# Attention scores in three float32r passes, with the operands cut beforehand and reciprocals spread by GpSimd

## The chip, the cores and the metric

The kernel runs on one core of one Trainium2 chip. The metric is the device time of one execution in microseconds (us). All times of the profile count from the start of its span. Engines go by the names of the profile: PE (TensorE, matmuls), PEld (its weight loads), DVE (VectorE), ACT (ScalarE), POOL (GpSimd) and SP (SyncE, which issues most DMAs).

## What is computed

One block of a transformer trunk in float32: 1024 latent tokens on a grid of 16 rows by 64 columns and 256 context tokens, width 1024. A modulated RMS norm is followed by a projection into a pooling half and queries, keys and values of 8 heads of 64. The attention, cut to what matters here, is

```python
s_loc = jnp.einsum('bnqhd,brnkhd->bhnqrk', q_r, k_b) * scale
s_loc = jnp.where(col_mask, s_loc + bias, -jnp.inf)      # 8 x 16 neighbourhood, learned bias
s_ctx = jnp.einsum('bnqhd,bkhd->bhnqk', q_r, k_ctx) * scale
p = softmax(concatenate([s_loc, s_ctx]))
o = p_loc @ v_local + p_ctx @ v_ctx
```

Then come the output projection with a gated residual, a second modulated norm and a squared-ReLU MLP of width 4096 with another gated residual.

## The kernel before

Nearly every large product is made of float32r matmuls: an operand x is cut into a high part (x rounded to float32r, a cast on ACT) and a low part (x minus the high part, a subtraction on DVE), and a product takes three passes, high by high, high by low, low by high (`three`, L198 to L200). The large products are further arranged in seven block products P1 to P7 in place of eight (`seventh`, `last_query`), whose results are combined on DVE and ACT (`kept_product`, L907 to L925). The exceptions are products of the attention, which run directly on float32 operands.

Ahead of the attention the projections of keys and queries run in 24 numbered steps, two per product; an order of instructions on each engine is fixed by the program text. The tables of biases (`tables(j)`, L869 on) are built on POOL: a DMA on SP's queue brings the windows of the learned biases (`U`), and twelve POOL operations of 128x128 (L883) subtract them from a mask, for the two heads of group j. The table of group 0 is built in step 20; that of group j + 1 in the iteration of unit (j, 2), all twelve operations at once.

The attention is a loop over 32 units (j, m): j is a pair of heads, m a tile of 128 queries (two grid rows). Unit number i is 8j + m. The loop is pipelined by hand; iteration i issues, in this order (each engine works in the order of the text):

- tables, weight loads, `weighed(i-4)` (L1070, DVE: values times reciprocals), and at fixed i other work of the block: `mod_gate` (i = 4), `column_sums` (i = 5 for `sc`, i = 8 for `sh`), `mixed_split` (i = 8, 16, 24), `weight_split` (i in `HALVES` = 12, 14, 20, 22 and later);
- `scores(i)` (L971 on): one matmul per head for the local keys (384 columns; 256 at the image edges m = 0 and 7) and one per head for the 256 context keys, L984. A head has 64 rows, and the two heads of a unit use the upper and the lower half of PE's rows. Then one DVE instruction per head (L998) adds the bias table and takes the minimum `nm` that the softmax needs;
- `turn(i-2)` (L1026): PE transposes. The first two are of `rb`, the reciprocals of the softmax sums spread over 64 columns per head; then come the probabilities. `fifth_kept` (ACT, L1040) copies the result of the first ones to `px`;
- the exponentials of unit i (ACT, L1007) around the copies of the turned probabilities to `pt` (L1045, one half on ACT, one on DVE);
- for i below 2, the last projection product of the queries (`last_query("P4", i)`);
- `share(i-1)`: the reciprocal of the sums (L1011) and its spread into `rb` (L1013), both on DVE;
- `values(i-3)` (L1060): PE.

`column_sums` (L620 on) sums a modulation row on PE, copies the result on ACT (L621), stores it to memory in four DMAs (`mod_out`, L253) and reads it back, spread over the partitions, in one DMA (L623). These DMAs are issued by POOL, and L623 waits there until the four have landed. Accumulating DMAs (`add_to`, L188) are issued by POOL too; they bring the results of finished heads together (`y`, `ss`, `f`).

The scores have two sets of two PSUM banks, so the scores of unit i + 1 can start on a head's bank only when L998 of that head of unit i is done.

## Time and profile before

| what | value |
|---|---|
| median of 3 runs | 1032.79 us (1032.4 to 1032.83) |
| span of the profiled execution | 1030.8 us, about 2 us less than the runs; its own time isn't among the shown ones |
| PE busy | 1017.8 us, 99% of the span |
| attention loop, from the first score to the output projection | 219 to 322.4 us |
| scores' matmuls, L984 | 128 in the program, 256 records, 4% of the chain that ended last |
| reciprocals and spreads, L1011 and L1013 | 32 each, on DVE, median 227 ns a spread |
| table operations on POOL, L883 | 48 |

A float32 matmul of the program appears as two records, one for each of its passes; a float32r matmul as one. Durations of matmuls overlap, since they are pipelined: what one takes of PE's time is read from the distance of two starts. In lists of groups, the columns are the line, the engine, the operation, output and inputs, the shapes and a count; then busy time and mean duration of one; then the idle time of the engine just ahead of them and who ended it. "L623 <-DMA gsc" in brackets with a time is a wait and what ended it.

### The profile page before, as it was taken

The numbers are of one execution on the slowest core, as the hardware profiler recorded it, in microseconds if no ns is written. First come the engines' busy times: TensorE is split into PE (matmuls) and PEld (weight loads), VectorE is DVE, ScalarE is ACT, GpSimd is POOL, SyncE is SP. The second block draws the span as 40 slices with busy tenths as digits, with TensorE's granted clock in tenths as the row PEclk, the third lists the DMA queues.
The fourth block names the chain that finished last, engine by engine and source line by source line (L and its number), as shares of the span: only waits on it lengthen the run. The fifth ranks groups of instructions, "written<-read, shape, count | busy, mean of one in ns | idle before, by whom it ended". The sixth has DMA issues, their size and how long they took to land.

```text
span 1030.8 us, 15588 instructions
## 1 busy us (share of the span) xinstructions
PE 1017.8 (99%) x5782; PEld 834.2 (81%) x5782; DVE 751.8 (73%) x1187; ACT 543.7 (53%) x941; POOL 110.7 (11%) x168
## 2 busy tenths in 40 slices
PE   8999999999999999999999999999999999999997
PEld 6788888877887888888888888888888888888885
DVE  5588767858996587878998887855766666547576
ACT  7573255328887556776655544555543334334431
POOL 3011200244311311310000000000000000000001
PEclk9999999999999999999999999999999999999999
DMA  9999798632337866795786666637967766555556
GB/s 343 332 255 338 246 265 296 204 86 80 72 95 194 203 180 200 253 237 168 267 269 210 204 210 214 205 122 241 327 220 271 248 226 220 202 180 189 176 182 211
DMA packets 123132, 222.68 MB, mean 216 GB/s; under 512 B 9456, under 2 KB 55152, under 8 KB 123056
## 3 DMA queue, kind: packets, MB, share of 16 engines
q1 hardware_dynamic: 96560, 171.14, 50.4%
q0 software_dynamic: 9360, 19.58, 9.5%
q10 hardware_dynamic: 17136, 30.97, 8.0%
q8 instruction: 45, 0.74, 0.3%
q14 instruction: 31, 0.25, 0.1%
HBM read 168.16 MB, written 52.45 MB: 214 GB/s over the span
## 4 chain that ended last, share of the span: by engine, by line
PE 95%; DMA 2%; ACT 1%; DVE 1%; issue 0%; SPq 0%; DVEq 0%; POOLq 0%; ACTq 0%
PE pu L449 4%; PE S L984 4%; PE pa L1060 3%; PE phv L198 3%; PE phz L198 3%; PE phx L198 3%; PE pyx L198 3%; PE phx L200 3%; PE phv L199 3%; PE phx L199 3%; PE pyx L199 3%; PE pyx L200 3%; PE pyv L199 3%; PE pyv L198 3%; PE pyz L199 3%; PE pyz L198 3%
## 5 line engine op out<-in xcount | busy, mean ns | idle before, releaser
L1007 ACT ACTIVATE sp<-sp,nm 128x640 f32<-128x640 f32 (+1 forms) x64 | 51.4, 803 | 20.0 <-DVE nm L998 19.6
L1577 ACT ACTIVATE c<-c 128x512 f32<-128x512 f32 x48 | 30.3, 632 | 47.0 <-DVE c L1697 28.2
L146 ACT CAST wpS<-S 128x512 fp32r<-128x512 f32 x64 | 38.7, 616 | 26.4 <-PE phv L200 9.2
L198 PE MATMUL phx<-thB,wpA 128*128 128x512 f32 x128 | 50.2, 392 | 0.0
L200 PE MATMUL phx<-thB,wpA 128*128 128x512 f32 x128 | 49.8, 389 | 0.0
L199 PE MATMUL phx<-tlB,wpA 128*128 128x512 f32 x128 | 49.8, 389 | 0.0
L152 DVE TENSOR_TENSOR wpS<-S,wpS 128x512 fp32r<-128x512 f32 x64 | 43.4, 685 | 8.3 <-ACT wpS L146 8.3
L998 DVE CUSTOM_DVE_ANT_0 sp<-S,tab 128x640 f32<-128x640 f32 (+1 forms) x56 | 42.9, 803 | 8.8 <-PE S L984 7.3
L1578 ACT ACTIVATE c<-c 128x512 f32<-128x512 f32 x48 | 30.3, 631 | 15.1 <-DVE sa L1660 12.3
L140 POOL TENSOR_TENSOR ry<-vy,nhalf 128x1 f32<-128x1 f32 x8 | 5.9, 740 | 280.7 <-DVE vy L138 280.7
L198 PEld LDWEIGHTS phx<-thB,wpA 128*128 128x128 f32 x128 | 24.0, 188 | 5.5 <-ACT s L1628 0.5
L984 PE MATMUL S<-kT,q 64*128 64x384 f32 (+1 forms) x128 | 27.9, 495 | 0.3 <-DVE nm L998 0.3
L200 PEld LDWEIGHTS phx<-thB,wpA 128*128 128x128 f32 x128 | 24.0, 188 | 5.0
L199 PEld LDWEIGHTS phx<-tlB,wpA 128*128 128x128 f32 x128 | 24.0, 188 | 4.9
L1060 PE MATMUL pa<-pt,v 128*64 128x128 f32 x352 | 25.9, 279 | 0.6 <-ACT px L1040 0.2
L1045 DVE COPY pt<-T 128x512 f32<-128x512 f32 x32 | 22.0, 686 | 5.5 <-PE T L1026 5.5
L198 PE MATMUL phv<-thT,wpA 128*128 128x512 f32 x64 | 25.1, 392 | 0.0
L198 PE MATMUL phz<-thB,wpS 128*128 128x512 f32 x64 | 25.0, 391 | 0.0
L200 PE MATMUL phv<-thT,wpA 128*128 128x512 f32 x64 | 24.9, 389 | 0.0
L199 PE MATMUL phv<-tlT,wpA 128*128 128x512 f32 x64 | 24.9, 389 | 0.0
L200 PE MATMUL phz<-thB,wpS 128*128 128x512 f32 x64 | 24.9, 389 | 0.0
L199 PE MATMUL phz<-tlB,wpS 128*128 128x512 f32 x64 | 24.9, 389 | 0.0
(1100 smaller groups left out, 3359.7 us busy)
## 6 DMA issues: line engine op xcount, KB each, us to landing
b<-in_w SPq DMA_DIRECT2D x64, 512.0 KB, 4.2
hrS<-hdS SPq DMA_DIRECT2D x32, 512.0 KB, 5.1
hrA<-hdA SPq DMA_DIRECT2D x24, 512.0 KB, 5.5
wm<-in_w_mod SPq DMA_DIRECT2D x16, 512.0 KB, 9.7
wa_0w<-in_w SPq DMA_DIRECT2D x16, 512.0 KB, 5.3
wa_1w<-in_w SPq DMA_DIRECT2D x16, 512.0 KB, 4.5
hdA<-c ACTq DMA_DIRECT2D x32, 256.0 KB, 2.8
hdS<-sa ACTq DMA_DIRECT2D x32, 256.0 KB, 2.7
```

What stands on the lines that cost most here:

```text
L146: nc.scalar.copy(hi, src)
L152: nc.vector.tensor_tensor(lo, src, hi.bitcast(F32), sub)
L198: nc.tensor.matmul(ps, ahi, bhi, start=first, stop=False, skip_group_check=more)
L199: nc.tensor.matmul(ps, ahi, blo, start=False, stop=False, skip_group_check=more)
L200: nc.tensor.matmul(ps, alo, bhi, start=False, stop=last, skip_group_check=more)
L449: nc.tensor.matmul(pus[b][j], wk(wgt, k, low, j * P, P), r, start=(k == 0 and n == 0), stop=(k == KT - 1 and n == 2))
L984: nc.tensor.matmul(S[e][:, c0 : c0 + keys.shape[1]], q[hs, cols], keys[hs], start=True, stop=True)
L998: nc.vector.tensor_tensor_reduce(out=to, in0=s, in1=bt, scale=1.0, scalar=BIG, op0=add, op1=ALU.min, accum_out=nm)
L1007: nc.scalar.activation(sp, sp, AF.Exp, bias=least[i, e], scale=-1.0, accum_out=sums[i][:, e : e + 1])
L1060: nc.tensor.matmul(pa[e * HD : (e + 1) * HD, cols], v[:, f : f + HD], turns[i][:, e, c] if c < 4 else fifths[i][:, :, (e + 1) * HD : (e + ...
L1577: nc.scalar.activation(r, src, AF.Relu)
L1578: nc.scalar.activation(r, r, AF.Square)
```

## The change

It has four parts.

1. The scores run in three float32r passes per part and head, in the order high query by high key, high by low, low by high, instead of one float32 matmul. The keys are cut in blocks of 512, so a unit whose local keys cross column 512 (m = 3 and 4) gets three parts instead of two, one of them 128 columns wide. The program has 432 score matmuls instead of 128.
2. The cuts of their operands are made ahead of the units: of the context keys (`kc`, 128x1024) after step 10, of the first keys and queries after steps 20 and 22, of six more blocks of 128x512 around the product P7 ahead of the loop, and of one in iteration 1, all with the cast on ACT and the subtraction on DVE; and of seven more on GpSimd, with a copy and a subtraction each, at the end of iterations 6, 7, 8, 9, 14, 15 and 16.
3. `share(i-1)` moves up into `scores(i)`, between the DVE instructions of the two heads, and the spread goes from DVE to GpSimd; the reciprocal stays on DVE.
4. `tables` becomes a generator: from iteration (j, 1) on it issues the DMA of `U`, and in each of the next four iterations three of the twelve table operations.

```diff
         def tables(j):
...
+            yield
...
+                    yield
...
+        def parts_of(to, j, b, small=False, engine=None):
+            name = f"{'k' if to is keys else 'q'}P{j}_{b}"
+            src = kT[j][:, b * 512 : (b + 1) * 512] if to is keys else qT[j][b]
+            t = whl.tile([P, 1024], F32R, tag="hl", name=name) if small else page(name, F32R)
+            hi, lo = to[j, b] = t[:, :512], t[:, 512:]
+            if engine is None:
+                split(src, hi, lo)
+            else:
+                engine.tensor_copy(hi, src)
+                engine.tensor_tensor(lo, src, hi.bitcast(F32), sub)
...
+                if step == 10:
+                    kcs += [page(f"kc{n}", F32R) for n in "hl"]
+                    split(kcp, *kcs)
+                if step == 20:
+                    parts_of(keys, 0, 0)
+                if step == 22:
+                    parts_of(queries, 0, 0, True)
...
-            for c0, keys in parts:
-                for e, hs in enumerate(heads):
-                    nc.tensor.matmul(S[e][:, c0 : c0 + keys.shape[1]], q[hs, cols], keys[hs], start=True, stop=True)
+            parts = local + [(512, ck)] if inner else [(0, ck)] + local
+            for c0, k in parts:
+                for n_q, n_k in ((0, 0), (0, 1), (1, 0)):
+                    for e, hs in enumerate(heads):
+                        nc.tensor.matmul(S[e][:, c0 : c0 + k[0].shape[1]], q[n_q][hs, cols], k[n_k][hs],
+                                         start=(n_q + n_k == 0), stop=(n_q == 1))
...
                 least[i, e] = nm
+                if e == 0 and i > 0:
+                    share(i - 1)
...
             nc.vector.reciprocal(ri, sums[i])
-            nc.vector.tensor_copy(shares[i].rearrange("p (e t) -> p e t", e=2),
+            nc.gpsimd.tensor_copy(shares[i].rearrange("p (e t) -> p e t", e=2),
...
+            early_parts = [(keys, 0, 1, True), (keys, 1, 0, True), (queries, 1, 0, True), (keys, 1, 1),
+                           (keys, 2, 0, True), (queries, 2, 0, True)]
+            for p in early_parts[:3]:
+                parts_of(*p)
             for j in range(2):
                 last_query("P7", j)
+                for p in early_parts[3 + 2 * j : 5 + 2 * j]:
+                    parts_of(*p)
+            parts_at = {1: (queries, 0, 1)}
+            parts_at.update({i: (to, j, b, j == 2, nc.gpsimd) for i, to, j, b in
+                             ((6, queries, 1, 1), (7, keys, 2, 1), (8, queries, 2, 1), (9, keys, 3, 0),
+                              (14, keys, 3, 1), (15, queries, 3, 0), (16, queries, 3, 1))})
+            coming_tables = iter(())
             for i in range(N + 4):
-                if i < N and units[i][1] == 2 and units[i][0] < 3:
-                    tables(units[i][0] + 1)
+                if i < N and units[i][1] == 1 and units[i][0] < 3:
+                    coming_tables = tables(units[i][0] + 1)
+                next(coming_tables, None)
...
-                if 0 < i <= N:
+                if i == N:
                     share(i - 1)
                 if 2 < i <= N + 2:
                     values(i - 3)
+                if i in parts_at:
+                    parts_of(*parts_at[i])
```

More of the change, by code (lines that the diff above doesn't have):

```diff
@@ L885, in tables @@
                             msk[0][:, a, i], uv[:, :, i * QC : (i + 1) * QC], sub)
+                    yield
         kT, qT = [None] * 4, [[None] * 2 for _ in range(4)]
+        keys, queries, kcs = {}, {}, []
+        def parts_of(to, j, b, small=False, engine=None):
[8 more added lines that the diff above has]
+                engine.tensor_tensor(lo, src, hi.bitcast(F32), sub)
         by_tile = lambda t: t.rearrange("p (m t) -> p m t", t=P)
@@ L948, in hybrid_block @@
                 if step == 20:
-                    tables(0)
+                    for _ in tables(0):
+                        pass
                 if step in (21, 22):
@@ L973, in scores @@
             o = 1 if m == 0 else 0
-            q = qT[j][m // 4]
+            q = queries[j, m // 4]
+            ck = [a[:, j * CTX : (j + 1) * CTX] for a in kcs]
             cols = slice((m % 4) * P, (m % 4 + 1) * P)
@@ L977, in scores @@
             S = [ps_s.tile([P, 1024], F32, tag="S", name=f"S{j}_{m}_{e}") for e in range(2)]
-            if inner:
-                parts = ((128, kT[j][:, (m - 1) * P : (m + 2) * P]), (512, kc[:, j, :]))
-            else:
-                parts = ((0, kc[:, j, :]), (256, kT[j][:, (m + o - 1) * P : (m + o + 1) * P]))
-            for c0, keys in parts:
-                for e, hs in enumerate(heads):
-                    nc.tensor.matmul(S[e][:, c0 : c0 + keys.shape[1]], q[hs, cols], keys[hs], start=True, stop=True)
+            t0, t1 = (m - 1, m + 2) if inner else (m + o - 1, m + o + 1)
+            at = 128 if inner else 256
+            local = []
+            for b in range(2):
+                b0, b1 = max(t0, 4 * b), min(t1, 4 * b + 4)
+                if b0 < b1:
+                    local.append((at + (b0 - t0) * P, [a[:, (b0 - 4 * b) * P : (b1 - 4 * b) * P] for a in keys[j, b]]))
+            parts = local + [(512, ck)] if inner else [(0, ck)] + local
[4 more added lines that the diff above has]
+                                         start=(n_q + n_k == 0), stop=(n_q == 1))
             halves = lambda a: a.rearrange("p (a b) -> p a b", a=2)
@@ L1009, in share @@
         def share(i):
-            ri = sm(f"ri_{i}", 2, 2)
+            ri = sm(f"ri_{i}", 2, 3)
             nc.vector.reciprocal(ri, sums[i])
             shares[i] = att.tile([P, P], F32, tag="ri", name=f"rb{i}", bufs=2)
-            nc.vector.tensor_copy(shares[i].rearrange("p (e t) -> p e t", e=2),
+            nc.gpsimd.tensor_copy(shares[i].rearrange("p (e t) -> p e t", e=2),
                                   ri.rearrange("p (e o) -> p e o", o=1).to_broadcast([P, 2, HD]))
```

## The prediction

> **What bounds the kernel now.** I read the page first, then the busy time by stretches of time, the chain of work that ended last, the instruction groups of the stretch that the change touches, and at last the time lines of POOL, DVE and PE in it.

> ```profile
> span 1030.8 us, 15588 instructions
> PE 1017.8 (99%) x5782; PEld 834.2 (81%) x5782; DVE 751.8 (73%) x1187; ACT 543.7 (53%) x941; POOL 110.7 (11%) x168
> ...
> PE 95%; DMA 2%; ACT 1%; DVE 1%; issue 0%; SPq 0%; DVEq 0%; POOLq 0%; ACTq 0%
> ```

> PE sets the end: it is busy for 99% of the span, and 95% of the chain that ended last is PE. So a saving counts only where PE has less to do, and a new wait costs its full length wherever PE meets it. The span is 1030.8 us and the median of the runs 1032.79; I keep those 2.0 us between them, so a change of the span is a change of the time.

> ```profile
> core 0: us, PE busy (x) PEld busy (x) DVE busy (x) ACT busy (x) POOL busy (x), PEclk, DMA share, GB/s
> 219.00:322.40 103.40, 102.68 (x1489) 81.53 (x1489) 87.81 (x258) 85.11 (x225) 34.92 (x63) 1.00 0.44 110
> 180.00:190.00 10.00, 10.00 (x46) 8.29 (x45) 10.00 (x13) 2.18 (x3) 0.00 (x0) 1.00 0.79 255
> 200.00:213.40 13.40, 13.40 (x61) 11.11 (x60) 8.96 (x12) 3.26 (x5) 9.84 (x18) 1.00 0.27 50
> 213.40:219.00 5.60, 5.60 (x27) 4.39 (x27) 1.44 (x3) 0.00 (x0) 0.00 (x0) 1.00 0.09 17
> ```

> The attention loop is the stretch from 219.0 to 322.4: PE works 102.68 of 103.40 us at full clock (1.00), DVE 87.81, ACT 85.11, and POOL 34.92. Its units follow each other in the chain like this (start, length, what):

> ```profile
> 240.65 1.28 PE S L984 x8
> 241.93 0.05 PE pa L1026
> ...
> 243.85 1.06 PE S L984 x8
> ...
> 250.42 1.28 PE S L984 x8
> 251.70 0.05 PE pa L1026
> 252.25 1.24 PE pa L1060 x20
> ...
> 275.52 1.28 PE S L984 x8
> ...
> 300.68 1.28 PE S L984 x8
> ...
> 322.37 0.43 PE pox L198
> ```

> Units 6, 7, 9, 17 and 25 start their scores at 240.65, 243.85, 250.42, 275.52 and 300.68; a group of eight takes 25.1 us. Within a unit PE runs scores (1.28 inner, 1.06 at an image edge), the turn of the unit two back, then the values of the unit three back (1.24). The turn begins with the spread reciprocals (`rb`), so T(4) starts at 241.93 and T(7) at 251.70.

> **The change, part by part.**

> *Scores.* The difference of the two lengths, 0.22 us, is 128 columns in two passes: 0.86 ns a column. An inner score has 640 columns, 1.10 us in two passes, which leaves 0.18 us fixed. What a float32r pass takes is seen just ahead of the loop:

> ```profile
> 213.30 0.39 PE L198 MATMUL pqv<-S3h,wQT3h 128*128 128x512 f32 x1
> ...
> 218.51 0.39 PE L200 MATMUL pqv<-S3h,wQT3l 128*128 128x512 f32 x1
> ```

> First and last of 24 such products, 23 starts in 5.21 us: 0.2265 each, 0.442 ns a column. Three passes of 640 columns make 0.85, with the fixed part 1.03; for 512 columns 0.68 and 0.86. That is the best case, 0.25 and 0.20 saved. Two more pairs of weight loads per part are not priced by a row; I take 0.04 to 0.05 for them, so 1.07 and 0.91: 0.21 and 0.15 saved. In units m = 3 and 4 the keys cross column 512 and a 128-wide part appears. The nearest row is the turn:

> ```profile
> 242.10 0.50 PE T L1026 x16
> ```

> Eight pairs of the two row halves, each with a 128-column weight load, in 0.50: 0.0625 a pair. With that for the narrow pieces the unit comes to 1.05 plus the extra loads, 1.18 taken, 0.10 saved. A group of eight then saves 4 x 0.21 + 2 x 0.15 + 2 x 0.10 = 1.34 us; bounds 0.6 (each new pair of loads half exposed) to 1.8. That presumes that the two heads' float32r passes run side by side as the fp32 ones do, which no row shows.

> [...]

> *What keeps PE from having all of it.* The scores' banks go round through DVE:

> ```profile
> 228.43 0.82 DVE L998 CUSTOM_DVE_ANT_0 sp<-S,tab 128x640 f32<-128x640 f32 x1 [0.25 <-PE S L984]
> 229.18 0.82 DVE L998 CUSTOM_DVE_ANT_0 sp<-S,tab 128x640 f32<-128x640 f32 x1
> ...
> 230.53 0.16 DVE L1011 RECIPROCAL ri<-su 128x2 f32<-128x2 f32 x1
> ...
> 229.32 1.33 PE L984 MATMUL S<-kT,q 64*128 64x384 f32 x3 [0.30 <-DVE nm L998]
> 230.07 0.70 PE L984 MATMUL S<-kcT,q 64*128 64x256 f32 x2
> ```

> The second head's scores of the next unit go on at 230.07, 0.89 after the second reduction starts (229.18). The change puts a reciprocal (0.16, some 0.19 to the next start) between the two reductions. The round becomes 0.75 + 0.19 + 0.89 and most of a score, 2.8 to 2.9 us. An inner unit needs 1.07 + 0.67 + 1.24 = 2.98 of PE, but the units after an image edge need less and gain little: about 0.3 lost per group. And ACT:

> ```profile
> L1007 ACT ACTIVATE sp<-sp,nm 128x640 f32<-128x640 f32 x48 | 39.8, 830 | 8.4 <-DVE nm L998 8.0
> L1007 ACT ACTIVATION_READ_ACCUMULATOR sp<-sp,nm 128x1 f32 x63 | 11.9, 189 | 0.0
> L1045 ACT COPY pt<-T 128x512 f32<-128x512 f32 x30 | 16.9, 564 | 0.0
> L1040 ACT COPY px<-pz 128x192 f32<-128x192 f32 x23 | 7.5, 325 | 0.0
> ```

> Two exponentials, their sums read out, a `pt` and two `px` are 2 x 0.83 + 2 x 0.19 + 0.56 + 0.65 = 3.25 us by durations, some 2.8 back to back. With a weight cast of about 0.5 beside them (units 8, 12, 14, 16, 20, 22, 24) ACT passes 2.98, and `px`, for which the values wait, comes 0.2 to 0.3 late. I count 0.45 saved per group with casts and 0.85 in the last, which has none.

> *Reciprocals spread by POOL.* DVE loses 0.23 us a unit, off the path. But POOL works in order, and its queue holds a wait just ahead of the spread:

> ```profile
> 238.68 1.91 POOL L253 DMA_DIRECT2D gsc<-accsc  x4 [2.17 <-ACT accsc L621]
> 242.22 0.93 POOL L623 DMA_DIRECT2D sc<-gsc  x1 [1.63 <-DMA gsc<-accsc]
> 248.28 1.95 POOL L253 DMA_DIRECT2D gsh<-accsh  x4 [5.14 <-ACT accsh L621]
> 253.14 0.92 POOL L623 DMA_DIRECT2D s<-gsh  x1 [2.91 <-DMA gsh<-accsh]
> 254.08 4.94 POOL L883 TENSOR_TENSOR tab<-msk,U 128x128 f32<-128x128 f32 x12
> 258.97 0.88 POOL L188 DMA_DIRECT2D y<-f  x1
> 259.58 1.18 POOL L188 DMA_DIRECT2D ss<-f  x1
> ```

> In iterations 5 and 8 `column_sums` stores a row in four DMAs and reads it back with L623, which waits on POOL for their landing. `share(4)` and `share(7)` stand behind that. A spread on POOL I take at 0.3 (0.23 on DVE, 0.46 for a table operation). L623 ends at 242.22 + 0.93 = 243.15, rb4 at 243.45; T(4) started at 241.93, so PE is held back to 1.5 later than before (2.1 from where the faster scores bring it). That lateness, less 0.1, moves the scores of unit 8 and ACT's `accsh`: the stores start near 249.7 instead of 248.28, then 1.95 + 2.91 + 0.92 + 0.3 put rb7 at 255.75. T(7) started at 251.70: **4.05 us late**. Of this, T(4)'s 1.5 is part.

> *Splits on POOL.* No row has one. Per 128x512:

> ```profile
> L883 POOL TENSOR_TENSOR tab<-msk,U 128x128 f32<-128x128 f32 x36 | 15.3, 459 | 17.2 <-DMA U<-in_rpb 17.2
> L215 POOL MEMSET acca<- 128x1024 f32 x1 | 1.0, 955 | 6.2 <-DVE d L152 6.2
> ```

> A table operation over 128 columns takes 0.459, four times that 1.84; half the memset 0.48. Subtraction between 1.45 and 1.84, copy between 0.48 and 1.5: I take 1.5 + 0.7 = 2.2, nearest to these rows. Those of units 6 and 7 end about 249.4, just ahead of the stores. Those of 8 and 9 stand ahead of rb8 and rb9, three table operations (1.35) ahead of rb9, three more and the additions of `y` and `ss` (0.6 to 1.2 each) ahead of rb10. Queued from 255.75: rb9 ready at about 262.1, wanted at 261.8; rb10 at 265.6, wanted at 265.1. With rounding 0.7 us more. Units 14 to 16 have POOL free.

> *Other edits, costed at nothing.* The cut of the context keys (step 10) meets a full DVE (180 to 190: 10.00 of 10), which is level with PE again by 200 (8.96 of 13.40); it costs up to 1.2 if a bank is waited for. The early cuts lie in P7, where DVE works 1.44 of 5.60 us and ACT not at all. The tables in steps come long before the group that needs them.

> [...]

> ```profile
> L1013 DVE COPY rb<-ri x32: 226/227/392, 228.0 to 327.0; 128x128 f32<-128x128 f32 x32
> ```

> It takes 227 ns, and up to 392 beside the table operations. [...]

> **Sum.** T(7) +4.05; T(9) and T(10) +0.7; the rest of group two, from unit 11, -0.4; group three -0.45; group four -0.85. Net +3.05: span 1033.85, time 1035.8.

> **Rivals.**

> *All the scores' saving arrives (same).* After the stalls DVE and ACT are ahead and PE sets the pace alone. Then 1.34 a group over 2.75 groups is 3.7, net +1.05: 1033.8. For it: PE's share of 99%. Against: ACT's 2.8 and a cast beside 2.98.

> *The scores stream and the landing is short (faster).* One price: L623 waits 1.63 for the second row as for the first (2.91), and no backlog. With both rows stored 0.6 sooner, as the quicker scores before them allow, T(7) is 2.2 late, and scores at their best, 1.8 a group over 2.75 groups, give 5.0 back: -2.8, 1030.0. It decides from a lateness at T(7) under about 2.9 (5.0 less 2.1). Against: the two waits differ in the trace itself, and loads must be wholly hidden.

> *POOL's splits are dear.* At 1.84 for each of the two operations, 3.7, those of units 6 and 7 push the stores by about 2 and those of 8 and 9 the spreads by 3 more: 1040.8.

> *The change doesn't do what it says.* If a 64-row float32r pass takes an fp32 pass's 0.86 ns a column, or the heads follow each other, three passes stand against two: +0.55 an inner unit, +0.44 an edge, some +17 over the loop: 1050. Nothing in the trace shows a float32r product on 64 rows.

> **How the numbers follow.** Forecast 0.43, all savings 0.22, streaming with a short landing 0.20, dear splits 0.10, slow passes 0.05. The range leaves out the slow passes and the outer part of the fast case: 1029.5 to 1041. A run of this kernel can tell about 0.2%, 2.1 us, from no change: 1030.7 to 1034.9 is same. Forecast and dear splits lie above, all savings within, the fast case just below: faster 0.20, same 0.22, slower 0.58.

> **What would show it.** Score pieces of 1.07 and 0.91 in the chain; PE idle before T(4) and T(7), released by `rb` on POOL, of about 2.1 and 3.3; POOL copies of 0.7 and subtractions of 1.5; T(7) near 255.75; 24.7 us from unit 17 to unit 25, and 20.8 (21.7 before) from there to the first `pox`. The forecast is wrong if POOL's spread is not behind L623, if a score takes over 1.28, or if the groups shrink by 1.3 or more.

## The result, and the profile after

The changed kernel takes 1037.68 us (median of 5 runs, 1036.72 to 1039.35) against 1032.62 us: a ratio of 1.0051, with a 95% interval of 1.0039 to 1.0064. It is 5 us slower. The forecast was 1035.8 with a range of 1029.5 to 1041.

The page of the kernel after shows a longer span with a PE that is busy for less time than before (1017.8 us then):

```profile
span 1035.9 us, 16106 instructions
...
PE 1015.6 (98%) x5958; PEld 842.6 (81%) x5958; DVE 752.6 (73%) x1165; ACT 549.0 (53%) x951; POOL 133.0 (13%) x214
```

So PE's work did shrink, and idle time took more than that. The list of what PE waited for in the loop (waiting operation, releaser, us in total, times, longest) names it:

```profile
PE pa L1057 <- POOL rb L1044: 5.1, 2, 3.0
PE pa L1091 <- ACT px L1071: 1.4, 5, 0.4
PE S L1012 <- DVE nm L1027: 0.9, 2, 0.5
```

Two waits for the spread reciprocals on POOL, 5.1 us together. POOL's time line shows what stands ahead of the two spreads:

```profile
238.44 1.95 POOL L253 DMA_DIRECT2D gsc<-accsc  x4 [0.58 <-ACT accsc L621]
243.12 0.94 POOL L623 DMA_DIRECT2D sc<-gsc  x1 [2.72 <-DVE nm L1027]
244.05 0.53 POOL L1044 COPY rb<-ri 128x128 f32<-128x128 f32 x2
244.52 0.62 POOL L901 CAST qP<-q 128x512 fp32r<-128x512 f32 x1
245.23 1.27 POOL L902 TENSOR_TENSOR qP<-q,qP 128x512 fp32r<-128x512 f32 x1
...
253.42 1.96 POOL L253 DMA_DIRECT2D gsh<-accsh  x4 [0.51 <-ACT accsh L621]
257.42 0.93 POOL L623 DMA_DIRECT2D s<-gsh  x1 [2.04 <-DMA gsh<-accsh]
258.35 0.30 POOL L1044 COPY rb<-ri 128x128 f32<-128x128 f32 x1
```

The read-backs L623 wait 2.72 and 2.04 us for their stores to land, and `rb` of unit 4 and of unit 7 follow only then. (The first wait is put down to `nm`. The four stores took up to 3.3 us to land, in this row of the tile `gsc`, so the last landing is the later event.)

```profile
DMA to landing us min/median/max: 1.6/2.9/3.3
```

The chain that ended last goes through both places (start, length, what):

```profile
244.41 0.37 PE pa L1057
...
244.99 0.85 PE T L1057 x13
245.85 2.33 PE pa L1091 x20
248.18 1.58 PE S L1012 x7
...
258.70 0.27 PE pa L1057
...
267.90 0.52 ACT wo_0h L1113
268.42 0.22 ACT px L1071
...
268.68 1.31 PE pa L1091 x20
...
282.72 1.08 PE S L1012 x12
...
307.03 1.07 PE S L1012 x12
...
315.70 1.25 PE S L1012 x18
...
324.89 0.91 PE S L1012 x11
...
327.73 0.43 PE pox L198
```

T(4) starts at 244.41 (241.93 before) and T(7) at 258.70 (251.70 before). From T(7) to the output projection it takes 69.03 us, 1.64 less than before (70.67). One thing is new: after the first wait the values take 2.33 us, where the same twenty records took 1.24. The stretches of time show why; the columns are those of the table by stretches in the prediction, with PE's granted clock third from the end:

```profile
241.30:244.40 3.10, 0.13 (x4) 0.00 (x0) 1.64 (x5) 0.16 (x2) 1.28 (x3) 0.91 0.47 167
244.40:246.00 1.60, 1.59 (x24) 1.47 (x26) 0.03 (x1) 0.97 (x3) 1.51 (x3) 0.50 0.15 3
...
250.00:252.00 2.00, 2.00 (x38) 1.81 (x34) 1.77 (x6) 1.89 (x6) 1.21 (x3) 0.83 0.10 37
...
258.70:262.00 3.30, 3.29 (x63) 3.06 (x64) 1.15 (x3) 2.54 (x8) 3.13 (x5) 1.00 0.09 1
```

After 2.98 us without a matmul the clock is 0.50, from 243.87 to 250.70. PE is "busy" there, at about half the pace (2.33 for 1.24). After the second wait, 2.10 us, it is 1.00.

### The profile page after: what moved, and what is told of

Its sections match the earlier page's. It is cut to its first block, busy times and chain, and to the rows that moved or that the text cites. A ratio compares the mean times of both kernels' runs of the same rounds, so it can differ in the third digit from the quotient of the medians.

```text
span 1035.9 us, 16106 instructions
## 1 busy us (share of the span) xinstructions
PE 1015.6 (98%) x5958; PEld 842.6 (81%) x5958; DVE 752.6 (73%) x1165; ACT 549.0 (53%) x951; POOL 133.0 (13%) x214
## 4 chain that ended last, share of the span: by engine, by line
PE 73%; ACT 1%; issue 1%; DVE 0%; POOL 0%; DMA 0%; POOLq 0%; DVEq 0%; ACTq 0%
PE phz L198 3%; PE phv L198 3%; PE phx L198 3%; PE pyx L198 3%; PE pa L1091 3%; PE phx L199 3%; PE pyx L200 3%; PE phx L200 3%; PE pyv L199 3%; PE phz L200 3%; PE pyz L199 3%; PE pyx L199 3%; PE phv L200 3%; PE pyz L198 3%; PE pyv L198 3%; PE phv L199 3%
## 5 line engine op out<-in xcount | busy, mean ns | idle before, releaser
L1622 ACT ACTIVATE c<-c 128x512 f32<-128x512 f32 x48 | 30.3, 632 | 44.3 <-DVE c L1742 25.1
L198 PE MATMUL phx<-thB,wpA 128*128 128x512 f32 x128 | 50.2, 392 | 0.0
L200 PE MATMUL phx<-thB,wpA 128*128 128x512 f32 x128 | 49.9, 389 | 0.0
L152 DVE TENSOR_TENSOR wpS<-S,wpS 128x512 fp32r<-128x512 f32 x64 | 43.4, 686 | 8.2 <-ACT wpS L146 8.2
L198 PEld LDWEIGHTS phx<-thB,wpA 128*128 128x128 f32 x128 | 24.0, 188 | 5.5 <-ACT s L1673 0.5
L200 PEld LDWEIGHTS phx<-thB,wpA 128*128 128x128 f32 x128 | 24.0, 188 | 5.0
L1012 PE MATMUL S<-kP,qP 64*128 64x256 f32 (+2 forms) x240 | 25.8, 324 | 0.9 <-DVE nm L1027 0.9
L198 PE MATMUL phz<-thB,wpS 128*128 128x512 f32 x64 | 25.0, 391 | 0.0
L198 PE MATMUL phv<-thT,wpA 128*128 128x512 f32 x64 | 25.0, 391 | 0.0
L200 PE MATMUL phz<-thB,wpS 128*128 128x512 f32 x64 | 24.9, 390 | 0.0
L199 PE MATMUL phy<-tlT,wpS 128*128 128x512 f32 x64 | 24.9, 389 | 0.0
L198 PE MATMUL phz<-thT,wpS 128*128 128x512 f32 x64 | 24.9, 389 | 0.0
```

The lines of the kernel that those rows point to most:

```text
L152: nc.vector.tensor_tensor(lo, src, hi.bitcast(F32), sub)
L198: nc.tensor.matmul(ps, ahi, bhi, start=first, stop=False, skip_group_check=more)
L199: nc.tensor.matmul(ps, ahi, blo, start=False, stop=False, skip_group_check=more)
L200: nc.tensor.matmul(ps, alo, bhi, start=False, stop=last, skip_group_check=more)
L1012: nc.tensor.matmul(S[e][:, c0 : c0 + k[0].shape[1]], q[n_q][hs, cols], k[n_k][hs], start=(n_q + n_k == 0), stop=(n_q == 1))
L1622: nc.scalar.activation(r, src, AF.Relu)
```

## The experiments

Theory A, from the prediction: the time is lost because the spreads stand behind a wait in POOL's queue. Its rivals are B, POOL has too much to do, and C, the scores and the reciprocal's new place cost time themselves. Each ratio is to the kernel before, run beside it, with its 95% interval.

### The read-backs moved away from the spreads

```diff
             mod_out(name, acc)
+
+        def column_read(name, to):
             nc.gpsimd.dma_start(to, gates[name].rearrange("o (k p) -> p (o k)", p=P))
...
+                if i == 7:
+                    column_read("sc", scale2)
+                if i == 10:
+                    column_read("sh", s2)
```

> The changed kernel with one thing moved: the two read-backs L623 go from the end of column_sums (iterations 5 and 8) to the ends of iterations 7 and 10, behind the spreads of units 4 to 6 and 7 to 9. Theory A (PE's two stalls, and the half clock after the first, come from the spread standing behind that wait on POOL): no PE wait for rb over 0.5 us, clock 1.00 all through the loop, T(7) about 1 us ahead of its place in the kernel before, 1029 to 1031 us. Theory B (POOL is simply too slow for spreads, splits and tables together): the waits for rb stay between units 4 and 10, 1035 us or more. Theory C (the scores and the reciprocal's new place cost time as well): no waits for rb, but 1032.6 or above.

1030.81 us, ratio 0.9974 (0.9965 to 0.9983). The wait list:

```profile
PE pa L1093 <- ACT px L1073: 1.2, 4, 0.4
PE S L1014 <- DVE nm L1029: 0.9, 2, 0.5
PE pa L1059 <- POOL rb L1046: 0.9, 2, 0.7
```

One short wait for `rb` is left (0.7, over the 0.5 that A allowed), POOL's backlog ahead of the spread of unit 10; the clock is 1.00 in all stretches. Two DMAs, moved to the ends of two later iterations, turn 5 us of loss into 2 us of gain. A holds; B accounts for less than 1 us, and C as a loss is out.

### Only the first read-back moved

```diff
-            nc.gpsimd.dma_start(to, gates[name].rearrange("o (k p) -> p (o k)", p=P))
+            if name == "sh":
+                nc.gpsimd.dma_start(to, gates[name].rearrange("o (k p) -> p (o k)", p=P))
...
+                if i == 7:
+                    nc.gpsimd.dma_start(scale2, gates["sc"].rearrange("o (k p) -> p (o k)", p=P))
```

> The changed kernel with only the first read-back (sc, iteration 5) moved to the end of iteration 7; the second (sh) stays ahead of the spread of unit 7. Stall theory: T(4) no longer waits and the clock stays at 1.00, T(7) still waits for about 2.5 us, about half of what the changed kernel lost against the run with both read-backs moved comes back: 1033 to 1035 us. If the half clock after the first stall were no part of it, the two stalls would be worth about 3 and 2 us and this would be 1034 to 1035; with it, 1032.5 to 1034.

1034.47 us, ratio 1.0015 (1.0006 to 1.0024): about half came back, but not in the way expected. (The time lies in the range given for a first stall without half clock, and misses the one with it; but the half clock moved to the other stall, so it decides nothing there.) PE's remaining wait, and the stretch behind it:

```profile
PE pa L1058 <- POOL rb L1045: 3.2, 1, 3.2
```

```profile
254.00:256.00 2.00, 1.49 (x22) 1.37 (x24) 0.20 (x1) 1.08 (x5) 1.91 (x4) 0.50 0.15 2
256.00:258.00 2.00, 2.00 (x22) 1.67 (x18) 0.49 (x1) 1.35 (x4) 1.92 (x4) 0.50 0.00 0
...
260.00:262.00 2.00, 2.00 (x37) 1.76 (x35) 2.00 (x6) 1.40 (x5) 0.96 (x3) 0.86 0.00 0
```

With T(4) on time, the second wait is longer, 3.2 us, and now the clock falls there. That the clock fell in the changed kernel is no matter of unit 4.

It is not the length of the wait alone either. 2.98 and 3.18 us of idle PE were followed by half clock and 2.10 was not; but in two runs further down 1.79 us was followed by it, and 2.47 us was not. Here are two stretches of the run with one pass, with the 1.79 us wait in the first, and three of the run with the spread on DVE, with the 2.47 us wait across the first two:

```profile
256.84:260.25 3.41, 1.62 (x36) 1.35 (x36) 2.18 (x7) 2.32 (x7) 3.41 (x9) 1.00 0.65 110
260.25:263.67 3.42, 3.42 (x42) 2.88 (x40) 2.24 (x7) 2.48 (x8) 1.29 (x4) 0.50 0.29 49
```

```profile
292.16:295.57 3.41, 2.37 (x46) 1.99 (x42) 3.03 (x4) 2.21 (x7) 3.26 (x8) 1.00 0.56 96
295.57:298.98 3.41, 1.98 (x41) 1.92 (x42) 2.91 (x6) 1.94 (x5) 1.79 (x4) 1.00 0.35 63
298.98:302.40 3.42, 3.42 (x63) 3.18 (x64) 3.36 (x12) 2.80 (x9) 0.00 (x0) 1.00 0.46 81
```

The stretches are cut so for a reason. In the traces here the pieces of half clock in the loop last 3.41 or 6.83 us (260.25 to 263.67 with one pass, 243.87 to 250.70 in the changed kernel), and between two of one run lies a whole number of times 3.413 us: 11 from start to start in the run with the spread on DVE (234.13 and 271.68), 229 in the changed kernel from the end of the piece, 250.70, to the next start, 1032.35, behind the last matmul. Cut into pieces of 3.41 us along that grid, the changed kernel has 2.44 us of idle PE in the piece just ahead of its half clock; its second wait is split into 0.92 and 1.18 us, and the clock stays at 1.00. In the stretches shown, a piece with 1.79 us of idle PE was followed by half clock, pieces with 1.04 and 1.43 were not. So a wait that lay inside one piece lowered the clock where a longer one, split over two, didn't.

### The spread, the reciprocal's place and the tables alone

The kernel before with parts 3 and 4 of the change; scores in float32, no splits.

> The kernel before with the reciprocal moved, the spread on GpSimd and the tables in steps; scores in float32, no splits. Theory A: PE waits for rb at T(4) (about 1.5 to 2.5 us) and at T(7) (about 2.5), nothing is given back: 1036 to 1038; the clock falls only if a stall reaches about 3 us. Theory B (the splits make the backlog): within 1 us of the kernel before.

1038.88 us, ratio 1.0053 (1.0041 to 1.0066): the whole loss without the float32r scores, and 0.9 us above the 1036 to 1038 expected. PE waits for `rb` twice, 4.5 us in all and 2.9 at the longest, and here too the clock falls once, behind the longer wait (0.55 in the stretch from 258 to 260, 0.60 from 260 to 262). That it takes a stall of about 3 us for that is shown by no run: 1.79 us were enough with one pass. B, in which the splits make the backlog, is refuted.

The same with both read-backs moved to the ends of iterations 7 and 10:

> The kernel before with the spread on GpSimd, the reciprocal between the reductions, the tables in steps and both read-backs moved, but the scores in float32 and no splits. What the float32r scores bring net is its distance to the same with them (1030.8 us). Theory: no wait for rb, within 0.5 us of the kernel before, so the scores bring about 2 us of the 4.6 that their shorter pieces add up to. If the gain of that run came from the spread alone: about 1031.

1032.87 us, ratio 0.9997 (0.9988 to 1.0005), and in the loop PE waits 0.4 us for `nm` and for nothing else. So the spread on POOL, its place and the tables in steps cost and bring nothing once the read-backs are out of the way, and the float32r scores bring 2 us net.

### The scores alone

All splits and the float32r scores; reciprocal and spread on DVE in their old place, tables in one go.

> The scores in float32r with all their splits, those on GpSimd too; reciprocal and spread on DVE where the kernel before has them, tables in one go. Theory A: 1029 to 1031, no stall. Theory C with the scores at fault: 1032.6 or above. With the reciprocal's place at fault instead: below the run that only brings the spread back to DVE by 1 us or more.

1032.32 us, ratio 0.9992 (0.9984 to 1.0001). The expected 1029 to 1031 did not come: the scores that bring 2 us with the spread on POOL bring nothing clear with it on DVE. PE waits 1.4 us for `nm` and 1.1 for `f`. The spread copy takes up to 1.19 us where POOL's splits run, which leads to the next two runs.

### The spread back on DVE

```diff
-            nc.gpsimd.tensor_copy(shares[i].rearrange("p (e t) -> p e t", e=2),
+            nc.vector.tensor_copy(shares[i].rearrange("p (e t) -> p e t", e=2),
```

> The changed kernel with the spread copy back on DVE, behind the reciprocal in its new place between the two reductions. Theory A: the stalls are gone, DVE's round for the scores' banks grows by 0.2 us a unit, which costs at most 0.1 us a unit where it binds: 1030 to 1032. Theory B: the same, since POOL is relieved. Theory C: 1033 or above, and the round of the banks is late in nearly every unit.

1044.54 us, ratio 1.0109 (1.0095 to 1.0123): 7 us slower than the change it was to mend. As a number it lies in theory C's "1033 or above", but no theory had the reason; the banks are late seven times, not in nearly every unit:

```profile
PE S L1012 <- DVE nm L1027: 8.4, 7, 2.5
```

Around one unit, DVE's time line and POOL's:

```profile
267.19 2.44 DVE L1044 COPY rb<-ri 128x128 f32<-128x128 f32 x1
269.56 0.81 DVE L1027 CUSTOM_DVE_ANT_0 sp<-S,tab 128x640 f32<-128x640 f32 x1
```

```profile
266.49 3.06 POOL L884 TENSOR_TENSOR tab<-msk,U 128x128 f32<-128x128 f32 x6
```

A copy of 0.23 us takes 2.44 and ends with the run of six table operations (269.63 and 269.55); the longest of this run takes 2.75. The second reduction, and with it the bank for the next scores, waits behind it. Two readings were left: the copy is held while POOL's run of operations lasts, or the place between the reductions is at fault. The fastest version below has the reciprocal behind both reductions; with its spread on DVE:

> The fastest version (read-backs, casts, tables and reciprocal all moved) with the spread copy back on DVE, behind both reductions. Port theory (the earlier run with the spread on DVE took 1044.5 us because a DVE copy that meets a run of GpSimd operations is held until that run ends): several spread copies of 1 to 2.8 us again, ending with a run of GpSimd operations, 1033 us or more. Place theory (it took so long because the copy stood between the two reductions): copies of 0.23 to 0.4, within 1 us of 1029.

1045.22 us, ratio 1.0115 (1.0098 to 1.0132), where the same with the spread on POOL takes 1028.97. The spread copies of this run (minimum, median, maximum in ns), one of them in DVE's time line, and POOL meanwhile:

```profile
L1046 DVE COPY rb<-ri x32: 226/227/5754, 226.2 to 342.7; 128x128 f32<-128x128 f32 x32
```

```profile
293.70 5.75 DVE L1046 COPY rb<-ri 128x128 f32<-128x128 f32 x1
```

```profile
293.20 1.89 POOL L886 TENSOR_TENSOR tab<-msk,U 128x128 f32<-128x128 f32 x3
294.42 1.22 POOL L1115 CAST wo_1h<-wor 128x512 fp32r<-128x512 f32 x1
294.99 3.02 POOL L886 TENSOR_TENSOR tab<-msk,U 128x128 f32<-128x128 f32 x6
297.39 1.17 POOL L1115 CAST wo_1h<-wor 128x512 fp32r<-128x512 f32 x1
297.96 1.79 POOL L886 TENSOR_TENSOR tab<-msk,U 128x128 f32<-128x128 f32 x3
```

The copy starts inside a run of twelve table operations and two casts, and ends near its end (299.45; the last ends at 299.75). In both runs every spread copy over 0.3 us overlaps operations or DMA issues of POOL. The place theory is out. The copy was held over a run of many instructions, up to 5.75 us; what in the chip holds it, no run shows.

### What takes the rest of the scores' gain

Three edits to the run with the read-backs moved, one at a time:

```diff
-        def high(src, hi, lo):
-            nc.scalar.copy(hi, src)
+        def high(src, hi, lo, on_pool):
+            (nc.gpsimd.tensor_copy if on_pool else nc.scalar.copy)(hi, src)
...
-            high(heads[j][:, :512], mp[:, :512], mp[:, 512:])
+            high(heads[j][:, :512], mp[:, :512], mp[:, 512:], j in (1, 2))
...
-            high(raw_o[0, kk][:, cs], hi[:, cs], lo[:, cs])
+            high(raw_o[0, kk][:, cs], hi[:, cs], lo[:, cs], n < 4)
```

> Both read-backs moved, and the six casts of iterations 12, 14, 16, 20, 22 and 24 go from ACT to GpSimd (0.61 us there as on ACT). If ACT is what keeps the faster scores from the end in those groups: px is no longer late, each of the two groups gains 0.5 to 1 us against both read-backs moved alone, 1029 to 1030. If the backlog of GpSimd or the banks' round keeps it: no gain, or up to 1 us slower.

```diff
-                next(coming_tables, None)
+                if not (8 < i < N and units[i][1] in (2, 3)):
+                    next(coming_tables, None)
```

> Both read-backs moved, and the table operations of groups 2 and 3 come two iterations later (m = 4 to 7), out of the stretch in which GpSimd has two splits, a read-back and two accumulating DMAs. If that backlog is what delays T(9) and T(10): the wait for rb (0.9 us) goes, 0.5 to 1 us faster than both read-backs moved alone. Otherwise within 0.3 us.

```diff
-                if e == 0 and i > 0:
+                if e == 1 and i > 0:
                     share(i - 1)
```

> Both read-backs moved, and the reciprocal issued after the reductions of both heads instead of between them. If the place between them lengthens the banks' round where it binds (m = 1 to 3): 0.5 to 1.2 us faster than both read-backs moved alone. If instead the place matters because it brings rb sooner: slower. If neither: within 0.3 us.

Their ratios are 0.9974 (0.9964 to 0.9984), 0.9979 (0.9970 to 0.9988) and 0.9978 (0.9969 to 0.9987): none can be told from 0.9974 without them, and the expected gains of 0.5 us or more each didn't come. The traces show the waits change places: with the casts on POOL none for `px` is in the list, with the tables later the one for `rb` falls from 0.9 to 0.2 us while that for `px` grows from 1.2 to 1.6. All three together:

> Both read-backs moved, the six casts on GpSimd, the table operations two iterations later and the reciprocal behind both reductions, together. If each takes away a separate wait (rb, px, the banks' round), their gains in the loop add up: some 1.2 us shorter than with the read-backs alone, 1029 to 1030 us. If they share one limit, no faster than the casts alone, 1030.3.

1028.97 us, ratio 0.9958 (0.9944 to 0.9971), about 4 us faster than the kernel before and the fastest full version here. (Its interval still overlaps that of the run with the read-backs alone, 0.9965 to 0.9983.) PE's list no longer has `px`; its first row is

```profile
PE pa L1059 <- POOL rb L1046: 1.6, 2, 1.1
```

How near the next limits are, the run with one pass instead of three shows:

```diff
-                for n_q, n_k in ((0, 0), (0, 1), (1, 0)):
+                for n_q, n_k in ((0, 0),):
```

> Both read-backs moved, and the scores in one float32r pass instead of three: the two passes with a low part are left out, so the scores have float32r's precision only. It takes about 0.6 us of PE's work from each of 32 units, 18 us in all. If PE sets the pace of the loop with room on the other engines: 1012 to 1016 us. If ACT (2.8 us a unit and more with a cast) or the banks' round through DVE is already next to it: a unit can't go below some 2.8, 1024 to 1028.

1026.78 us, ratio 0.9937 (0.9923 to 0.9950). The 18 us of PE's work were an estimate; PE's busy time on the two pages falls by 11.2 us, from 1013.9 with the read-backs moved to 1002.7, and the time by 4. The waits that took the place of the work are spread over all three engines, and 3.41 us run at half clock (the stretch at 260.25 shown above):

```profile
PE pa L1059 <- POOL rb L1046: 3.1, 3, 1.8
PE pa L1093 <- ACT px L1073: 1.9, 5, 0.5
PE pa L1059 <- DVE f L1103: 1.5, 5, 0.4
PE S L1014 <- DVE nm L1029: 1.1, 2, 0.6
```

## Why the prediction was right, and where it was off

*The mechanism* held: PE waits at T(4) and at T(7) for spreads that stand behind the landing of a store in POOL's queue, and taking that away removes the loss.

*The size at T(7)* was off: 4.05 us late was forecast, 7.00 measured. This is the mis-sized term, in two parts. The stores of `sc` landed later: L623 waited 2.72 us, not the 1.63 of the kernel before, so T(4) came at 244.41 instead of 243.45. Behind that wait of 2.98 us the clock was 0.50, for which the sum has no term. The pieces there took 2.33 for 1.24 (values), 1.58 for 0.91 (scores) and 0.85 and, at 250.07, 0.80 for 0.50 (turns), 2.4 us in all, and pushed the stores of `sh` from the forecast 249.7 to 253.42. Their landing was 0.87 shorter than taken, hence T(7) came 2.95 after its forecast place (258.70 against 255.75) and not 3.7. The prediction did not weigh a fall of the clock; the kernel before shows none in its loop (1.00 from 219 to 322.4), and with one pass 1.79 us without a matmul within one piece of 3.41 us were enough for it.

*T(9) and T(10)* did not wait for `rb`: 0.7 us had been counted. A split on POOL took 0.62 + 1.27 = 1.89 us instead of 2.2, and a spread 0.29. From T(7) to unit 17 it still took 24.02 us where the kernel before took 23.82; 0.3 longer had been forecast. The chain shows the casts there (the row of `wo_0h` at 267.90, then `px`, then the values); the chain of the kernel before has such a cast as well, at 267.37, so they alone don't explain the length.

*The later groups* saved more than forecast: 24.31 us from unit 17 to unit 25 (24.7 forecast, 25.16 before) is 0.85 saved and not 0.45; 20.70 from there to the first `pox` (20.8; 21.69 before) is 0.99 and not 0.85.

*The sum.* Against the forecast, T(7) is 2.95 later, the way to unit 17 0.10 shorter, the two later groups 0.40 and 0.14 shorter, and what follows the loop 0.26 shorter: 2.05 in all, which is the 5.1 us of the span against 3.05. That the time lies inside the range is in part luck: the upper bound came from dear splits, and what used the room was a half clock that the sum did not have.

*The scores' pieces* came as forecast in most units: 1.08 for 1.28, 0.91 for 1.06. In unit 28 (m = 4) the piece is 1.25: 0.03 saved, not 0.10. So the narrow part costs more than the row of the turn, 0.0625 us a pair, let expect (1.25 for the 1.18 taken). The 0.04 to 0.05 us that the sum took for two more pairs of weight loads a part is shown by no run, since none takes the loads apart from the rest of the piece; the runs show the whole pieces, 1.08 and 0.91 where 1.07 and 0.91 were forecast. For m = 3 the piece saves nothing in the changed kernel: 1.35 in unit 19, where the kernel before has 1.28. The others add up to 16 x 0.20 + 8 x 0.15 + 4 x 0.03 = 4.5 us. Of these 2 arrive with the read-backs moved (1030.81 against 1032.87 with float32 scores), and about 4 is the distance with casts, tables and reciprocal moved too, though no float32 version with these three moves was run. In the changed kernel they are all but hidden by the waits: 1.0051 with them, 1.0053 without.

*The rivals.* Slow float32r passes on 64 rows did not come: the two heads' passes run side by side, 1.08 us for an inner piece, where one head behind the other would come to 1.70 (six passes of 640 columns at the 0.442 ns a column of the prediction). Dear splits did not come (1.89 us each). Of the rival "the landing is short" half came: the second wait was 2.04 us instead of 2.91, but the first was 2.72 instead of 1.63.

What stays open: what each of casts, tables and reciprocal is worth alone; how much idle time within 3.41 us lowers the clock (1.43 us did not and 1.79 did, in the stretches shown); and why the stores of `sc` landed late. While they landed, a weight load moved 360 GB/s (242 to 243 us), where the kernel before moves 16. L623 waited 2.72 and 2.90 us beside such a load (the changed kernel, the scores alone) and 1.63 without (the kernel before, the spread alone). But for `sh` it waited 3.02 us in the run with the spread alone, with 14 GB/s at 252 to 254 us, and no run moves the load.

## What to carry to other kernels

Before work is moved to an engine's queue, read that queue around the new place: here two DMAs that waited 2.72 and 2.04 us for another's landing held the spreads behind them, and moving the two changed the sign of the whole edit. A stall of PE cost more than its length, because half clock followed: behind 2.98 us the pieces took 2.4 us longer. And a saving on the bounding engine is worth only the distance to the next limit: of 11 us of PE's busy time taken away, 4 came through.

## What had not been expected of the hardware

A spread copy on DVE that met a run of GpSimd operations was held, in the two examples above until the run was over or nearly so: 0.23 us became 2.44 and 5.75 us. Beside the run of twelve table operations in the kernel before it had taken 0.39 at most; why that one let it in sooner isn't known. With splits, tables and casts on GpSimd, the spread was better off on GpSimd too: 1028.97 against 1045.22 us.
